# 48 instead of 40 tokens through the row experts of a hybrid decoder layer, one-hots in one operation, parts of p made earlier

## The chip, the cores and the metric

The kernel runs on one core of a Trainium2 chip. The metric is device time in microseconds (us) of one execution; lower is better. The kernel before took 2658.15 us, the median of three runs (2655.53 to 2660.96).

## What is computed

One layer for 264 tokens (256 of a prompt, 8 samples) of width 2048, in fp32. Two mixers (a chunked SSD scan and a short gated convolution) and their projections give x1; then each token goes through a product-key expert layer, and at the end a gate with a projection of p:

```python
def peer(x, w_q, keys1, keys2, u_tab, v_tab):
    q = (xt @ w_q).reshape(n, PEER_HEADS, 2, PEER_DKEY // 2)
    t1, i1 = lax.top_k(einsum(q[:, :, 0], keys1), 16)
    t2, i2 = lax.top_k(einsum(q[:, :, 1], keys2), 16)
    ...
    top, pos = lax.top_k(cand, 16)
    gate = softmax(top)
    hid = gelu(einsum('td,thkd->thk', x, u_tab[idx]))
    return einsum('thk,thkd->td', gate * hid, v_tab[idx])

x2 = LN(ALPHA * x1 + peer(x1))
y = x2 + sigmoid(x2 @ ple_gate_w) * (p @ ple_proj_w)
```

There are 8 heads, 128 x 128 = 16384 experts, each one row of u and one of v, and every token picks 16 experts per head, 128 in all.

## The kernel before

Every product is made from a high and a low part (fp32r) of both operands: `split_w` (L138) casts a half block of weights to `whi` on ACT and subtracts it to `wlo` on DVE (L146), three half blocks ahead (LOOK). A weight block is two halves of 512 KB each, fetched on the SP queue. `col_block` serves plain projections with three matmuls of 264 columns for each of 16 weight tiles.

The experts are reached in two ways. For the first TD = T - NSP = 224 tokens all 16384 experts are computed: `pair_block` (L260) streams, for each of 16 weight tiles, 448 columns (high and low parts side by side) against `whi` and the 224 high ones against `wlo`. 128 such blocks over u give hidden values, which go to DRAM as `a_d` (`u_evac`); 128 over v, in 8 chunks of 16 blocks, multiply coefficients `co` into accumulators (`v_evac`). The gate of each token and expert is built as a matrix of 128 x 128 by one-hots: `gates` (L1138) makes, for four tokens, `o1` on POOL (L1150) and `o2` on DVE (L1151); `g_mm` multiplies them and ACT gathers 32 tokens in `gs`, which goes to DRAM as `g_d`. Before each v chunk, `prep` (L1278) loads `gl` from `g_d` and `al` from `a_d` for four sets k, multiplies them on DVE (L1288), casts on ACT (L1296) and subtracts on DVE (L1297) to make `co`. The first of them can only begin when all gates are made, since `to_v` (L1340) closes the pools of the selection and of the one-hots before it opens the pool for v.

For the other NSP = 40 tokens (32 of the prompt's end and the 8 samples) `sparse_experts` (L1178) gathers the rows themselves: 128 rows at a time, one gather per token slot and table, 40 of u and 40 of v. DVE multiplies a gathered tile `ug` with `x1s` (L1206), and later accumulates v rows into `x1s` (L1216). Tokens come in groups GR, of 32 and of 8; at a group's end 16 small matmuls with `fld` fold the rows (`yS`, L1222), and the next group's `x1s` is loaded from `x1_d` (L1201).

What sets the order: the program is written out by hand. Main loops issue blocks; `tick` (L162) after each half block runs background tasks, generators that yield their cost in us of DVE, in the order of the list `tasks`, until the tick's budget is used, or `("w", n)` to sleep n ticks. `defer` runs a function n ticks later. `Grid(n)` makes a task come back every n ticks: every 3 for a group of four gates, every STEP = 4 for a gathered row. `select_all` (L1086) selects for three sets of tokens t = 0, 1, 2 (the prompt's second half, the samples, the prompt's first half), sends the indices of the row tokens to DRAM (`send`), spawns `sparse_experts` after t = 1 and the gates of the second half after t = 0. A v chunk whose `co` are not yet issued makes the program run ticks without a block (`run_out`). At the end the parts of p (`pp`) come from `quad`, four buffers that `co` of every second chunk, the last one too, also uses.

```python
    def quad(name, dt=R):
        return pairs.tile([128, 8 * TW], dt, name=name, tag="pr", bufs=KB // 4)
...
            if c % 2:
                co = quad("co")[:, 0:8 * TD]
...
    pp = quad("pp")[:, 0:4 * T].rearrange("p (q a t) -> p q a t", q=2, a=2)
```

Of the kernel before, what the change touches and what calls it, by code (L numbers as in the profile page):

```python
# [10 lines left out]
F = mybir.dt.float32  # L11
R = mybir.dt.float32r
# [9 lines left out]
TW = T + 2  # L22
NSP = 40
TD = T - NSP
# [21 lines left out]
TB = 32  # L46
NB = TD // TB
GR = ((0, 32), (32, 8))


@with_exitstack
def hybrid_step(ctx: ExitStack, tc: tile.TileContext, xT, pT, w_in, w_dt, w_bs, w_bc, w_o, w_q, w_pg, w_pp,
# [1033 lines left out]
    def select_all():  # L1086
# [26 lines left out]

    sx_d = [dram.tile([128, n], U32, name=f"sx{g}_d") for g, (_, n) in enumerate(GR)]
    sg_d = [dram.tile([128, n], F, name=f"sg{g}_d") for g, (_, n) in enumerate(GR)]
    x1_d = dram.tile([NSP, D], F, name="x1_d")

    def send(sel, t, nh):

        k0, m = GR[t]  # L1120
# [6 lines left out]
        lo, hi = (n - m, n) if t == 0 else (0, n)  # L1127
        r, c = hi - lo, nh * TOPK // m

        def out(d):  # L1130
            return bass.AP(tensor=d.tensor, offset=d.offset, ap=[[m, r], [r * m, c], [1, m]])

        gp.dma_start(out=out(sx_d[t]), in_=ix[lo:hi].rearrange("p (c m) -> p c m", m=m))
        gp.dma_start(out=out(sg_d[t]), in_=sel[lo:hi, 2].rearrange("p (c m) -> p c m", m=m))

    GS = {}

    def gates(t0, n):  # L1138
        oh = P["oh"]
        grid = Grid()  # L1140
        for tt in range(t0, t0 + n, 4):
            b0, q0 = divmod(tt, TB)
            if q0 == 0:
                GS["t"] = oh.tile([128, 128, TB], F, name="gs", tag="gs", bufs=2)
            gs = GS["t"]
# [7 lines left out]
            if q0 + 4 == TB:  # L1153
                defer(8, lambda gs=gs, b0=b0: sy.dma_start(out=g_d[b0], in_=gs))
            yield 1.1
            yield grid(3)
# [21 lines left out]
    def sparse_experts():  # L1178
        jobs = [(tab, k0, n, c) for k0, n in GR for tab in (uR, vR) for c in range(k0, k0 + n)]
        rows = {}  # L1180

        def get(i):
            if i < len(jobs):
# [4 lines left out]
                rows[i] = t  # L1188

        yield ("w", 1)  # L1190
        for g, (k0, n) in enumerate(GR):
            gp.dma_start(out=sidx[:, k0:k0 + n], in_=sx_d[g])
            gp.dma_start(out=scf[:, k0:k0 + n], in_=sg_d[g])
# [77 lines left out]
    def load(k):  # L1271
        gl = vp.tile([128, NB, 4, TB], F, name="gl", tag="gl", bufs=2)
        gp.dma_start(out=gl, in_=g_d[:, :, 4 * k:4 * k + 4, :].rearrange("b p e t -> p b e t"))
        al = vp.tile([128, 4, TD], F, name="al", tag="al", bufs=2)
        gp.dma_start(out=al, in_=a_d[k])
        AL[k] = (al, gl)

    def prep(c):  # L1278

        for k in range(4 * c, 4 * c + 4):  # L1280
# [83 lines left out]
    for c in range(ECH):  # L1364
# [88 lines left out]
def _inputs(x_prompt, x_sample, p_prompt, p_sample, state_ssm, state_ssd_conv, state_shortconv,  # L1453
# [70 lines left out]
```

## Time and profile before

| | before |
|---|---|
| median of three runs | 2658.15 us |
| the profiled execution | 2656.88 us |
| its span, first to last instruction | 2655.1 us |
| TensorE busy (matmuls) | 2617.6 us, 99% |
| DVE busy | 2017.8 us, 76% |
| ACT busy | 1347.8 us, 51% |
| POOL busy | 621.7 us, 23% |
| HBM read and written | 616.93 and 41.87 MB, 248 GB/s |

Shares are means over stages with different loads, so the stages have to be looked at one by one. Times in the trace are us from the first instruction. The u blocks run from about 1145 to 1858, the v blocks from there to 2532, the projection of p and the statistics to 2554 and the last projection to the end. Matmuls are pipelined: their spans overlap, and the spacing of their starts is the time that each one takes. PE is TensorE, PEld its weight loads.

### The profile page before, as it was taken

How to read it: one execution, taken by the hardware profiler on the slowest of the kernel's cores; microseconds unless marked ns; L12 is line 12 of the kernel's file. 1: busy time of each engine (PE TensorE's matmuls, PEld its weight loads, DVE VectorE, ACT ScalarE, POOL GpSimd, SP SyncE). 2: the span in 40 equal slices, each digit the busy share in tenths (PEclk: the TensorE clock that was granted, in tenths of full speed). 3: DMA queues.
4: the chain of work that ended last, by engine and by line, in shares of the span. 5: the costliest groups of instructions: out<-in, count | busy, mean ns of one | idle time of the engine just before them, and what ended most of it. 6: DMA issues, size and time to landing. Idle time of an engine off the chain costs nothing.

```text
span 2655.1 us, 48788 instructions
## 1 busy us (share of the span) xinstructions
PE 2617.6 (99%) x18983; PEld 2539.3 (96%) x18983; DVE 2017.8 (76%) x3371; ACT 1347.8 (51%) x1896; POOL 621.7 (23%) x743
## 2 busy tenths in 40 slices
PE   8999999999999999999999999999899999999999
PEld 8999999999999999999999999999899989999989
DVE  8899965556445567899997777778889889776976
ACT  5665533454344445654656555556444434444563
POOL 2232200000000010100356686742232222000100
PEclk9999999999999999999999999999999999999999
DMA  7798755555655555566778898889999999877654
GB/s 236 214 303 269 245 170 179 181 169 189 182 178 181 181 177 178 178 194 201 230 240 314 304 334 320 313 326 383 365 360 366 335 335 372 279 249 235 201 172 134
DMA packets 198601, 662.02 MB, mean 249 GB/s; under 512 B 22472, under 2 KB 59960, under 8 KB 186936
## 3 DMA queue, kind: packets, MB, share of 16 engines
q1 hardware_dynamic: 156128, 510.17, 58.0%
q0 software_dynamic: 24224, 129.62, 13.3%
q10 hardware_dynamic: 18016, 19.10, 2.1%
q8 instruction: 148, 2.42, 0.4%
q14 instruction: 85, 0.70, 0.1%
HBM read 616.93 MB, written 41.87 MB: 248 GB/s over the span
## 4 chain that ended last, share of the span: by engine, by line
PE 88%; DVE 6%; issue 3%; DMA 2%; POOL 1%; ACT 0%; SPq 0%; DVEq 0%; POOLq 0%; ACTq 0%
PE mm L270 25%; PE mm L236 14%; PE mm L234 14%; PE mm L235 14%; PE mm L271 13%; DVE wlo L146 2%; PE mm L273 2%; PE gps L1162 2%; DMA w<-uT 0%; DMA al<-a_d 0%; DVE x1s L1216 0%; DMA x1s<-x_d 0%; POOL ug L1186 0%; DVE acc L1323 0%; PE scr L994 0%
## 5 line engine op out<-in xcount | busy, mean ns | idle before, releaser
L146 DVE TENSOR_TENSOR wlo<-w,whi 128x1024 fp32r<-128x1024 f32 x916 | 1118.0, 1224 | 438.6 <-ACT whi L145 435.7
L145 ACT CAST whi<-w 128x1024 fp32r<-128x1024 f32 x916 | 961.5, 1051 | 822.1 <-PE mm L235 288.6
L270 PE MATMUL mm<-co,whi 128*128 128x448 f32 x1920 | 620.1, 377 | 6.7 <-DVE co L1297 6.7
L270 PE MATMUL mm<-x,whi 128*128 128x448 f32 x1920 | 620.5, 378 | 0.0
L236 PE MATMUL mm<-x,wlo 128*128 128x264 f32 x1920 | 549.6, 286 | 2.7 <-DVE wlo L146 2.7
L234 PE MATMUL mm<-x,whi 128*128 128x264 f32 x1920 | 549.5, 286 | 0.2 <-ACT whi L145 0.2
L235 PE MATMUL mm<-x,whi 128*128 128x264 f32 x1920 | 547.1, 285 | 0.0
L271 PE MATMUL mm<-co,wlo 128*128 128x224 f32 x2048 | 529.8, 269 | 6.6 <-DVE wlo L146 6.6
L271 PE MATMUL mm<-x,wlo 128*128 128x224 f32 x2048 | 525.3, 267 | 4.0 <-DVE wlo L146 4.0
L271 PEld LDWEIGHTS mm<-co,wlo 128*128 128x128 f32 x2048 | 394.5, 193 | 11.5 <-DVE wlo L146 7.6
L271 PEld LDWEIGHTS mm<-x,wlo 128*128 128x128 f32 x2048 | 392.4, 192 | 8.5 <-DVE wlo L146 5.4
L270 PEld LDWEIGHTS mm<-co,whi 128*128 128x128 f32 x1920 | 365.4, 190 | 36.3 <-DVE co L1297 8.1
L270 PEld LDWEIGHTS mm<-x,whi 128*128 128x128 f32 x1920 | 362.0, 189 | 28.1 <-ACT sv L996 0.5
L236 PEld LDWEIGHTS mm<-x,wlo 128*128 128x128 f32 x1920 | 362.0, 189 | 3.2 <-DVE wlo L146 3.1
L234 PEld LDWEIGHTS mm<-x,whi 128*128 128x128 f32 x1920 | 363.0, 189 | 1.9 <-issue 1.4
L235 PEld LDWEIGHTS mm<-x,whi 128*128 128x128 f32 x1920 | 363.2, 189 | 0.0
L1150 POOL TENSOR_SCALAR o<-iot,slot,slot 128x128 f32<-128x128 f32 x224 | 277.8, 1249 | 73.6 <-PE gps L1162 69.3
L1186 POOL DMA_INDIRECT ug<-vR,sidx x40 | 70.6, 1766 | 256.8 <-DVE x1s L1216 207.9
L832 POOL CAST r1h<-r1gbh 128x2 fp32r<-128x2 f32 x16 | 5.2, 328 | 476.3 <-PE mm L236 476.3
L1256 ACT COPY as<-mm 128x224 f32<-128x224 f32 x128 | 43.9, 343 | 115.0 <-PE mm L273 115.0
L1206 DVE SCALAR_TENSOR_TENSOR ug<-ug,x1s 128x2048 f32<-128x2048 f32 x40 | 91.4, 2284 | 8.0 <-DMA x1s<-x_d 8.0
L1186 POOL DMA_INDIRECT ug<-uR,sidx x40 | 62.9, 1571 | 140.0 <-DVE ug L1206 130.6
(348 smaller groups left out, 3904.2 us busy)
## 6 DMA issues: line engine op xcount, KB each, us to landing
w<-uT SPq DMA_DIRECT2D x256, 512.0 KB, 4.9
w<-vP SPq DMA_DIRECT2D x256, 512.0 KB, 5.9
w<-w_in SPq DMA_DIRECT2D x240, 512.0 KB, 3.7
w<-w_bc SPq DMA_DIRECT2D x32, 512.0 KB, 3.5
w<-w_bs SPq DMA_DIRECT2D x32, 512.0 KB, 3.5
w<-w_o SPq DMA_DIRECT2D x32, 512.0 KB, 3.5
w<-w_q SPq DMA_DIRECT2D x32, 512.0 KB, 3.6
w<-w_pg SPq DMA_DIRECT2D x32, 512.0 KB, 4.2
```

The costliest lines, as they stand in the source:

```text
L145: ac.copy(hi, w)
L146: ve.tensor_tensor(lo, w, hi.bitcast(F), OP.subtract)
L234: te.matmul(ps, wh, xh[kb], start=(first and q == 0), stop=False)
L235: te.matmul(ps, wh, xl[kb], start=False, stop=False)
L236: te.matmul(ps, wl, xh[kb], start=False, stop=(last and q == n - 1))
L270: te.matmul(ps, hi[:, ws], xp[kb], start=(kb == 0), stop=False)
L271: te.matmul(ps[:, :TD], lo[:, ws], xp[kb][:, :TD], start=False, stop=False)
L273: te.matmul(ps, hi[:, ws], xp[kb], start=False, stop=True)
L1150: gp.tensor_scalar(o1[:, q], iot, slot[0][:, c], slot[2][:, c], OP.is_equal, OP.mult)
L1162: te.matmul(ps[:, q * 128:(q + 1) * 128], o2[:, q], o1[:, q], start=True, stop=True)
L1186: gp.indirect_dma_start(out=t, out_offset=None, in_=tab, in_offset=bass.IndirectOffsetOnAxis(ap=sidx[:, c:c + 1], axis=0))
L1206: ve.scalar_tensor_tensor(t, t, 1.0, x1s, OP.mult, OP.mult, accum_out=shid[:, c:c + 1])
```

## The change

NSP becomes 48, so TD is 216: six blocks of 32 tokens and one of 24 (TR), which get a DRAM tile of their own (`gr_d`). GR gets a third group of 8; a group now names its selection (0 or 1) and its rows in it. The 48 row tokens are the prompt's last 40 and the 8 samples. `sparse_experts` is put at the head of the tasks at the end of selection 0, and waits for the samples' indices before its 33rd gather. `o2` for four tokens is one operation, and the yield behind it is 0.7 and not 1.1. The parts of p are made by a task that is spawned with the last v chunk, in buffers of the row experts.

```diff
-NSP = 40
+NSP = 48
...
-NB = TD // TB
-GR = ((0, 32), (32, 8))
+NB, TR = divmod(TD, TB)
+GR = ((0, 32, 0, 88, 32), (32, 8, 0, 120, 8), (40, 8, 1, 0, 64))
...
-            if t == 1:
-                spawn(sparse_experts())
+            if t == 0:
+                tasks.insert(0, {"gen": sparse_experts(), "wait": clock["t"] + 1})
...
-                ve.tensor_scalar(o2[:, q], iot, slot[1][:, c], None, OP.is_equal)
+            ve.tensor_tensor(o2, iot[:, None, :].to_broadcast([128, 4, 128]),
+                             slot[1][:, tt:tt + 4, None].to_broadcast([128, 4, 128]), OP.is_equal)
...
-            yield 1.1
+            yield 0.7
             yield grid(3)
...
+            if i == 32:
+                while "sent1" not in DONE:
+                    yield ("w", 1)
+                index(1)
             get(i + 1)
...
-        gl = vp.tile([128, NB, 4, TB], F, name="gl", tag="gl", bufs=2)
-        gp.dma_start(out=gl, in_=g_d[:, :, 4 * k:4 * k + 4, :].rearrange("b p e t -> p b e t"))
+        gl = vp.tile([128, 4 * TD], F, name="gl", tag="gl", bufs=2)
+        m = gl[:, 0:4 * NB * TB].rearrange("p (b e t) -> p b e t", b=NB, e=4)
+        r = gl[:, 4 * NB * TB:].rearrange("p (e t) -> p e t", e=4)
+        gp.dma_start(out=m, in_=g_d[:, :, 4 * k:4 * k + 4, :].rearrange("b p e t -> p b e t"))
+        gp.dma_start(out=r, in_=gr_d[:, 4 * k:4 * k + 4, :])
...
-            ve.tensor_tensor(av, av, gl.rearrange("p b e t -> p e b t"), OP.mult)
+            ve.tensor_tensor(av, av, m.rearrange("p b e t -> p e b t"), OP.mult)
+            ve.tensor_tensor(ar, ar, r, OP.mult)
...
+    def ple_parts():
+        pi = lp.tile([128, D], F, name="pi", tag="ug", bufs=2)[:, 0:2 * T].rearrange("p (q t) -> p q t", q=2)
+        gp.dma_start(out=pi, in_=pT)
+        pp = lp.tile([128, D], R, name="pp", tag="x1s", bufs=1)[:, 0:4 * T].rearrange("p (a q t) -> p a q t", q=2, a=2)
+        yield ("w", 4)
+        ac.copy(pp[:, 0], pi)
+        ve.tensor_tensor(pp[:, 1], pi, pp[:, 0].bitcast(F), OP.subtract)
...
             while "sparse" not in DONE:
                 tick(1.1)
+            spawn(ple_parts())
...
-    pp = quad("pp")[:, 0:4 * T].rearrange("p (q a t) -> p q a t", q=2, a=2)
-    for q in range(2):
-        t = block("pin")
-        gp.dma_start(out=t, in_=pT[:, q, :])
-        ac.copy(pp[:, q, 0], t)
-        ve.tensor_tensor(pp[:, q, 1], t, pp[:, q, 0].bitcast(F), OP.subtract)
```

Since a task list sets the order, these edits move instructions on every engine. Three places follow, with the names' buffer numbers.

POOL at the start of the gathers, before: behind selection 1 and behind 15 groups of `o1` (the last one stands here), the indices of both groups are loaded, then the first gather `ug` and the rows `x1s` are issued. L1150 is `o1`, L1192 and L1193 are the loads of the indices and gates, L1186 is a gather.

```order
L1150 TENSOR_SCALAR o1_17414<-iot_77,slot0_14370,slot2_14372 128x128 x4
L1192 DMA sidx_84<-sx0_d_13063 128x32
L1193 DMA scf_85<-sg0_d_13065 128x32
L1192 DMA sidx_84<-sx1_d_13064 128x8
L1193 DMA scf_85<-sg1_d_13066 128x8
L1186 DMA ug_17458<-uR,sidx_84 128x2048
L1201 DMA x1s_17460<-x1_d_13067 32x2048 x4
```

And in the change, where L1132 are the writes of the indices, L1188 is a gather and L1151 is `o1`:

```order
L1132 DMA sg1_d_13068<-sel0_15349 8x16x8
L1195 DMA sidx_84<-sx0_d_13064 128x32
L1196 DMA scf_85<-sg0_d_13067 128x32
L1195 DMA sidx_84<-sx1_d_13065 128x8
L1196 DMA scf_85<-sg1_d_13068 128x8
L1188 DMA ug_16027<-uR,sidx_84 128x2048
L1207 DMA x1s_16029<-x1_d_13070 32x2048 x4
L1188 DMA ug_16034<-uR,sidx_84 128x2048
L1151 TENSOR_SCALAR o1_16075<-iot_77,slot0_14373,slot2_14375 128x128 x4
```

The gathers stand ahead of the first `o1` of all, directly behind the writes of the indices that they read.

DVE at the seam from u to v, before: from the last block over u (L1257) to the first one over v (L1321). L1297 makes a `co`, L1216 adds a gathered row, L1288 multiplies `al` by `gl`.

```order
L1257 TENSOR_TENSOR as_22125<-mm_22129,as_22125 128x224
L1297 TENSOR_TENSOR co_22178<-al_21855,co_22178 128x4x224
L1216 SCALAR_TENSOR_TENSOR x1s_17460<-ug_22067,scf_85,x1s_17460 128x2048
L1288 TENSOR_TENSOR al_22071<-al_22071,gl_22069 128x896
L1297 TENSOR_TENSOR co_22191<-al_22071,co_22191 128x4x224
L1216 SCALAR_TENSOR_TENSOR x1s_17460<-ug_22176,scf_85,x1s_17460 128x2048
L146 TENSOR_TENSOR wlo_22201<-w_22152,whi_22200 128x1024
L146 TENSOR_TENSOR wlo_22227<-w_22198,whi_22226 128x1024
L1321 SCALAR_TENSOR_TENSOR acc_21527<-acc_21527,mm_22197 128x448
```

In the change the same stretch begins so (L1267 for L1257, L1301 and L1302 for L1288, L1311 for L1297, L1226 for L1216):

```order
L1267 TENSOR_TENSOR as_21940<-mm_21944,as_21940 128x216
L1301 TENSOR_TENSOR al_21883<-al_21883,gl_21880 128x4x192
L1302 TENSOR_TENSOR al_21883<-al_21883,gl_21880 128x4x24
L1226 SCALAR_TENSOR_TENSOR x1s_16029<-ug_21878,scf_85,x1s_16029 128x2048
L1311 TENSOR_TENSOR co_22009<-al_21883,co_22009 128x4x216
L1226 SCALAR_TENSOR_TENSOR x1s_16029<-ug_21991,scf_85,x1s_16029 128x2048
L1301 TENSOR_TENSOR al_21996<-al_21996,gl_21993 128x4x192
L1302 TENSOR_TENSOR al_21996<-al_21996,gl_21993 128x4x24
L1311 TENSOR_TENSOR co_22034<-al_21996,co_22034 128x4x216
L1226 SCALAR_TENSOR_TENSOR x1s_16029<-ug_22007,scf_85,x1s_16029 128x2048
```

The third and the fourth `co` follow in the same three rows, with one L1226 between them and one behind, and then two `wlo` and the first v block. All four of the first chunk's `co` stand behind the last u block; before, it was the difference of the third and the fourth.

DVE at the switch to the new third group of rows, in the change, at the end of the third v chunk (L1337 adds a v block, L1237 takes the folded group, L1216 multiplies the first rows of the next by the new `x1s`):

```order
L1337 TENSOR_TENSOR acc_22053<-mm_24458,acc_22053 128x432
L1311 TENSOR_TENSOR co_24509<-al_24261,co_24509 128x4x216
L1237 SCALAR_TENSOR_TENSOR x1sp_83<-x1sp_83,yS_24504 128x16x8
L147 TENSOR_TENSOR wlo_24548<-w_24481,whi_24547 128x1024
L1216 SCALAR_TENSOR_TENSOR ug_24358,shid_86<-ug_24358,x1s_24525 128x2048
L147 TENSOR_TENSOR wlo_24571<-w_24545,whi_24570 128x1024
```

Before, only the switch from the group of 32 to that of 8 stands there.

## Rows read from the trace of the kernel before

**Rows 1.** Stretches: window, length, busy us of PE, PEld, DVE, ACT, POOL, clock, DMA, GB/s.

```profile
650.00:700.00 50.00, 50.00 (x413) 50.00 (x412) 22.56 (x21) 19.73 (x22) 0.00 (x0) 1.00 0.59 180
...
1250.00:1300.00 50.00, 47.85 (x296) 45.24 (x295) 46.14 (x79) 28.44 (x40) 8.29 (x9) 0.97 0.72 231
...
1800.00:1850.00 50.00, 49.38 (x314) 46.79 (x313) 40.11 (x42) 32.02 (x48) 13.36 (x11) 1.00 1.01 391
...
2000.00:2050.00 50.00, 49.80 (x315) 47.07 (x315) 45.97 (x40) 22.72 (x22) 15.25 (x12) 1.00 0.93 361
...
GB/s 236 214 303 269 245 170 179 181 169 189 182 178 181 181 177 178 178 194 201 230 240 314 304 334 320 313 326 383 365 360 366 335 335 372 279 249 235 201 172 134
```

**Rows 2.** Waits of PE, whole span: us in total, times, longest.

```profile
PE mm L271 <- DVE wlo L146: 10.6, 7, 4.4
PE mm L270 <- DVE co L1297: 6.7, 5, 3.8
```

**Rows 3.** Timeline of PE in the tail: start, us, instruction, [idle before <- releaser].

```profile
2532.12 0.37 PE L273 MATMUL mm<-co,whi 128*128 128x448 f32 x1
...
2538.57 0.59 PE L1391 MATMUL mm<-pp,whi 128*128 128x264 f32 x1 [6.08 <-ACT pp L1378]
...
2554.10 0.29 PE L234 MATMUL mm<-r,whi 128*128 128x266 f32 x1
```

**Rows 4.** Timeline of DVE and PE at the seam from u to v.

```profile
1858.73 1.08 DVE L1297 TENSOR_TENSOR co<-al,co 128x896 fp32r<-128x896 f32 x1
1859.73 2.35 DVE L1216 SCALAR_TENSOR_TENSOR x1s<-ug,scf,x1s 128x2048 f32<-128x2048 f32 x1
1861.99 1.09 DVE L1288 TENSOR_TENSOR al<-al,gl 128x896 f32<-128x896 f32 x1
1864.09 1.09 DVE L1297 TENSOR_TENSOR co<-al,co 128x896 fp32r<-128x896 f32 x1 [1.00 <-ACT co L1296]
...
1859.87 0.47 PE L270 MATMUL mm<-co,whi 128*128 128x448 f32 x1 [1.08 <-DVE co L1297]
...
1865.23 0.74 PE L270 MATMUL mm<-co,whi 128*128 128x448 f32 x1 [3.84 <-DVE co L1297]
```

**Rows 5.** Timeline of PE in a u block, with one group of gates.

```profile
1700.94 0.26 PE L271 MATMUL mm<-x,wlo 128*128 128x224 f32 x1
1701.04 0.38 PE L270 MATMUL mm<-x,whi 128*128 128x448 f32 x1
1701.25 0.27 PE L271 MATMUL mm<-x,wlo 128*128 128x224 f32 x1
1701.35 1.06 PE L1162 MATMUL gps<-o,o 128*128 128x128 f32 x8
1702.17 0.46 PE L270 MATMUL mm<-x,whi 128*128 128x448 f32 x1
```

**Rows 6.** Timeline of PE at the group switch (last matmuls of v blocks, fold matmuls).

```profile
2110.61 3.65 PE L1222 MATMUL yS<-fld,x1s 128*128 128x32 f32 x32
...
2120.58 0.37 PE L273 MATMUL mm<-co,whi 128*128 128x448 f32 x1
...
2125.65 0.38 PE L273 MATMUL mm<-co,whi 128*128 128x448 f32 x1
...
2133.10 0.56 PE L271 MATMUL mm<-co,wlo 128*128 128x224 f32 x1 [4.36 <-DVE wlo L146]
...
2137.19 0.60 PE L273 MATMUL mm<-co,whi 128*128 128x448 f32 x1
...
2277.66 0.96 PE L1222 MATMUL yS<-fld,x1s 128*128 128x8 f32 x8
```

**Rows 7.** Timeline of DVE and POOL at the same switch.

```profile
2129.61 2.29 DVE L1206 SCALAR_TENSOR_TENSOR ug<-ug,x1s 128x2048 f32<-128x2048 f32 x1 [7.99 <-DMA x1s<-x_d]
...
2114.56 4.03 POOL L1201 DMA_DIRECT2D x1s<-x_d  x8 [17.36 <-PE yS L1222]
```

**Rows 8.** Landing times of the loads of `al` (L1275) and of gathers (L1186).

```profile
DMA to landing us min/median/max: 3.3/10.4/14.0
...
DMA to landing us min/median/max: 6.9/9.2/15.6
```

More of the change, by code (lines that the diff above doesn't have):

```diff
@@ L954, in hybrid_step @@
     g_d = dram.tile([NB, 128, 128, TB], F, name="g_d")
+    gr_d = dram.tile([128, 128, TR], F, name="gr_d")
     DONE = {}
@@ L1111, in select_all @@
         yield from gates(0, PT // 2)
-    sx_d = [dram.tile([128, n], U32, name=f"sx{g}_d") for g, (_, n) in enumerate(GR)]
-    sg_d = [dram.tile([128, n], F, name=f"sg{g}_d") for g, (_, n) in enumerate(GR)]
+    sx_d = [dram.tile([128, n], U32, name=f"sx{g}_d") for g, (_, n, _, _, _) in enumerate(GR)]
+    sg_d = [dram.tile([128, n], F, name=f"sg{g}_d") for g, (_, n, _, _, _) in enumerate(GR)]
     x1_d = dram.tile([NSP, D], F, name="x1_d")
     def send(sel, t, nh):
-        k0, m = GR[t]
         sp = P["sp"]
@@ L1126, in send @@
         ve.tensor_copy(ix[:n], fx[:n])
[L1127 to L1134, printed above, removed]
+        for g, (_, m, tile_, lo, r) in enumerate(GR):
+            if tile_ == t:
+                c = nh * TOPK // m
+                for d, src in ((sx_d[g], ix), (sg_d[g], sel[:, 2])):
+                    gp.dma_start(out=bass.AP(tensor=d.tensor, offset=d.offset, ap=[[m, r], [r * m, c], [1, m]]),
+                                 in_=src[lo:lo + r].rearrange("p (c m) -> p c m", m=m))
+        DONE["sent%d" % t] = True
     GS = {}
@@ L1142, in gates @@
             b0, q0 = divmod(tt, TB)
+            tb = TB if b0 < NB else TR
             if q0 == 0:
                 GS["t"] = oh.tile([128, 128, TB], F, name="gs", tag="gs", bufs=2)
-            gs = GS["t"]
+            gs = GS["t"].rearrange("p e t -> p (e t)")[:, 0:128 * tb].rearrange("p (e t) -> p e t", t=tb)
             o1 = oh.tile([128, 4, 128], F, name="o1", tag="o1", bufs=3)
@@ L1150, in gates @@
                 gp.tensor_scalar(o1[:, q], iot, slot[0][:, c], slot[2][:, c], OP.is_equal, OP.mult)
-                ve.tensor_scalar(o2[:, q], iot, slot[1][:, c], None, OP.is_equal)
+            ve.tensor_tensor(o2, iot[:, None, :].to_broadcast([128, 4, 128]),
+                             slot[1][:, tt:tt + 4, None].to_broadcast([128, 4, 128]), OP.is_equal)
             defer(6, lambda o1=o1, o2=o2, gs=gs, q0=q0: g_mm(o1, o2, gs, q0))
-            if q0 + 4 == TB:
-                defer(8, lambda gs=gs, b0=b0: sy.dma_start(out=g_d[b0], in_=gs))
-            yield 1.1
+            if q0 + 4 == tb:
+                defer(8, lambda gs=gs, b0=b0: sy.dma_start(out=g_d[b0] if b0 < NB else gr_d, in_=gs))
+            yield 0.7
             yield grid(3)
@@ L1178, in sparse_experts @@
     def sparse_experts():
-        jobs = [(tab, k0, n, c) for k0, n in GR for tab in (uR, vR) for c in range(k0, k0 + n)]
+        jobs = [(tab, k0, n, c) for k0, n, _, _, _ in GR for tab in (uR, vR) for c in range(k0, k0 + n)]
         rows = {}
@@ L1188, in get, with index @@
                 rows[i] = t
+        def index(t):
+            for g, (k0, n, tile_, _, _) in enumerate(GR):
+                if tile_ == t:
+                    gp.dma_start(out=sidx[:, k0:k0 + n], in_=sx_d[g])
+                    gp.dma_start(out=scf[:, k0:k0 + n], in_=sg_d[g])
         yield ("w", 1)
-        for g, (k0, n) in enumerate(GR):
-            gp.dma_start(out=sidx[:, k0:k0 + n], in_=sx_d[g])
-            gp.dma_start(out=scf[:, k0:k0 + n], in_=sg_d[g])
+        index(0)
         get(0)
@@ L1338, in residual @@
                 yield ("w", 1)
+    def ple_parts():
[5 more added lines that the diff above has]
+        ve.tensor_tensor(pp[:, 1], pi, pp[:, 0].bitcast(F), OP.subtract)
+        for q in range(2):
+            p_h.append(pp[:, 0, q])
+            p_l.append(pp[:, 1, q])
+        yield 0.7
     def to_v():
@@ L1488, in _inputs @@
         iota=np.tile(np.arange(128, dtype=np.float32), (128, 1)),
-        fold=np.concatenate([np.tile(np.eye(n), (128 // n, 1)) for _, n in GR], 1).astype(np.float32),
+        fold=np.concatenate([np.tile(np.eye(g[1]), (128 // g[1], 1)) for g in GR], 1).astype(np.float32),
     )
```

8 lines of the change are left out of this document (3 added, 5 removed).

## Prediction

> **What bounds the kernel now.** I read the busy time of stretches first. In the stretch of plain projections TensorE is busy for all of 50.00 us and issues 413 matmuls of 264 columns, 0.121 us each, with DVE at less than half [rows 1]. In the expert stages it is busy nearly all the time too, but with company: DVE 46.14 and 45.97 of 50 us in the stretches at 1250 and 2000, the DMA engines at 0.93 to 1.01 of their time with 361 to 391 GB/s from 1800 on [rows 1]. Then what TensorE waits for: over the whole span 10.6 us for DVE's low parts of the weights and 6.7 us for DVE's coefficients `co` [rows 2]; the other large wait, 6.08 us, stands in the tail [rows 3]. So this kernel is bound by TensorE's columns, with DVE and the DMA engines close behind in the expert stages. Fewer columns are worth their full time wherever DVE and DMA keep up, and every place where TensorE runs out of prepared operands costs its wait and then some: after the 3.84 us wait the first 448-column matmul shows 0.74 us and not 0.38 [rows 4, 5], which is the lower of the clock's two levels, 1.2 and not 2.4 GHz.
>
> **Columns.** TD falls from 224 to 216, so each `pair_block` streams 16 x (432 + 216) columns and not 16 x (448 + 224): 384 fewer. In order of time, a 448-column matmul is followed after 0.21 us, a 224-column one after 0.10 us [rows 5], and a whole block takes 5.07 us (2120.58 to 2125.65, [rows 6]), 0.47 ns a column, much as the 264-column stretch gives (0.121 us / 264 = 0.46 ns). By proportion a block loses 5.07 x 24 / 672 = 0.181 us; there are 128 blocks over u and 128 over v, so **-46.3 us**. The bounds: 0.417 ns a column, which is 2.4 GHz, gives -41; only the 16 columns of the wide matmul counting gives -31 (a rival below). I take the proportional price because three widths lie on one line through zero.
>
> **Gates.** 54 groups of four tokens and not 56. A group holds TensorE from 1701.35 to 1702.17, 0.82 us [rows 5]: **-1.6 us**. The one `o2` operation in place of four lies on DVE in a stretch in which nothing waits for it; I cost it at nothing, and the yield that falls from 1.1 to 0.7 only lets the other tasks have more of a tick.
>
> **Parts of p.** Now the last v matmul starts at 2532.12, and the p projection waits 6.08 us for its operand: the tile comes from the same four buffers as `co` of the last chunk, so the load cannot start before the last v block has ended. The out projection begins at 2554.10 [rows 3], 21.8 us after the last v matmul has streamed its 0.21 us. The work between is 96 matmuls at 0.121 us and four of the statistics, about 12.6 us. With the parts made at the start of the last chunk, in two tiles that the row experts have left, TensorE goes straight on: **-9.2 us**, the wait and the low clock behind it. Next late would be the statistics, issued after three of the four quarters of the projection, some 9 us after the last block; DVE and ACT need about 5 us for the last block's chain, so I expect no new wait. Bounds: 0 to -10.
>
> **The third group of row tokens.** 48 rows are 96 gathers and not 80. In the program's order they begin with the first selection's end, and the last is issued at the same v block as before (chunk 4, block 9); so the load on DVE and the DMA engines in the v stage stays as it is, and the extra 16 lie in the u stage, 2.3 us of DVE each, in ticks that have room (they come out of the same budget). But a group has fixed costs. The switch from the group of 32 to that of 8 shows them: DVE sits 7.99 us for the rows `x1s`, which POOL writes with 16 DMAs that can only start when the group's matmuls have read the old tile [rows 7]; TensorE runs out of low parts for 4.36 us, and the block takes 11.54 us (2125.65 to 2137.19), 6.5 over [rows 6]. The new third group adds one more such switch, with the gathered product again directly behind the tile's load on DVE, and one more set of fold matmuls in four pieces of 0.95 us [rows 6]. **+10.3 us**; bounds +4 (the fold alone) to +13.
>
> **The seam from u to v.** This is where the change loses. Selection and gates now share their budget with the gathers, so the last gates end 22 ticks later in the program and the pools for v open 20 ticks later: 6 half blocks before u ends, not 26. Before, three of the first chunk's four `co` were made by then, and TensorE waited 1.08 and 3.84 us for the rest, behind one gathered row and one product [rows 4]. In the new order all four stand between the last u block and the first v block on DVE, with four gathered rows among them. DVE alone: four row operations 4 x 2.26 (1859.73 to 1861.99), four products 4 x 1.2 (the split of `gl` into two adds some 0.2), four differences of 1.0, three waits of 1.0 for ACT's cast [rows 4] = 20.8 us, where 6.4 stand now (1858.73 to 1865.1). So at least +14.5. But the second, third and fourth loads each wait for a buffer or for POOL, which is held by a gather that waits for DVE; gathers land 9.2 us after issue, coefficients 10.4 (medians; 6.9 and 3.3 at best [rows 8]). With 8 us for a load, since the weights pause, and 7.5 for a gather, the last `co` comes some 29 us after the last u block, +22; with 11.4 us a load, +28. I take **+20 us**, the low clock at the restart included, nearer to the waits than to DVE's bare sum since the DMA engines were full in this stretch [rows 1].
>
> **DVE with less slack.** Blocks get 3.6% shorter, DVE's work does not, and the first gather now goes out directly behind the indices it needs, so DVE will stand for the first rows, as it did for 7.99 us at the switch [rows 7], of which half reached TensorE. **+4 us** for all of this, between 0 and +10.
>
> Sum: -46.3 - 1.6 - 9.2 + 10.3 + 20 + 4 = -22.8 against the profiled execution's 2656.9 us, 2634; the median of the three runs is 1.3 higher, so I say **2635 us**. A measurement of this kernel can tell about 0.2%, 5.3 us, from no change.
>
> **Rivals.**
> - *Weight loads set the pace of the narrow matmuls.* 32 matmuls of only 32 columns (f32) took 3.65 us, 0.114 each [rows 6]: there the columns are not what counts. If fp32r has a floor at the 0.10 us which the 224-column matmuls show, 216 columns are no faster and a block gains 16 x 16 x 0.47 ns only, -31 in all: **2651**. Against it: 0.10 for 224 and 0.121 for 264 lie in the ratio of the columns. The Trainium skill, page "TensorE: Matmul & The Clock Gate", section "LDWEIGHTS (loading the stationary operand)", gives a load about P/1.2 ns, 107 ns for 128 columns, which is this rival's floor; the spacing of 0.10 us in the rows is already slightly below it, so the trace speaks rather against.
> - *The seam is short*: loads land as at their best and DVE's bare sum rules, +14, and DVE's slack suffices: **2625**.
> - *The seam is long*, +28, and each restart drags the next blocks, +6: **2649**.
> - *The DMA engines become the bound in v (slower).* While gathers run, a block needs two weight halves of 0.52 MB, half a gather of 1.05 MB and a quarter of 0.88 MB of coefficients: 1.79 MB. At 4.89 us that is 367 GB/s, where the v stretch now shows 361 at 0.93 [rows 1]. Chunks 0 to 4 are 80 blocks; 14.5 us of the gain lie there. Without it the sum is -8.3, so the change loses from 5.17 us a block on, a limit of 346 GB/s. At 335 GB/s, the lowest two slices of the v stage on the page [rows 1], a block would take 5.36, +23: **2672**. Against it: 391 GB/s at 1.01 [rows 1].
>
> **How the numbers follow.** Forecast 0.50, weight floor 0.13, short seam 0.15, long seam 0.13, DMA bound 0.09. Faster by over 0.2% means below 2653: the forecast, the short seam and most of the weight floor and the long seam, 0.83. Within 0.2%: what is left of these two, 0.08. Slower: the DMA bound, 0.09. The range reaches from the low edge of the short seam (seam +12, no allowance, second switch +8), 2616, to the high edge of the long one and the foot of the DMA case, 2658.
>
> **What would show it.** A v block at 4.89 us between undisturbed last matmuls, and u blocks likewise; 204 and 100 ns between starts. If the narrow one stays at 0.10 and above and the block at 4.95, the floor is there. A wait of TensorE for `co` of 15 to 28 us in sum at the seam; two waits of DVE for `x1s` near 8 us in the v stage, each with some 4 us of TensorE behind it; no wait for `pp`. The prediction is wrong if v blocks in chunks 0 to 4 spread beyond 5 us with `whi` waiting for weights (DMA), if the seam costs no more than now, or if new waits for `wlo` appear all through the u stage, where I put the extra gathers at nothing.

## The result and the profile after

The change makes the kernel slower: 2682.06 us (median of four runs, 2679.95 to 2686.26) against 2659.36 us (four runs of the kernel before on the same chip, 2655.53 to 2660.96), a ratio of 1.0089, 95% interval 1.0072 to 1.0107. The forecast was 2635, a gain of 0.9%. The profiled execution took 2681.55 us, its span 2679.8, 24.7 more than the span before.

Its page and its waits of TensorE (us in total, times, longest; line numbers of the changed kernel, where L271 is the matmul against `whi`, L272 the one against `wlo`, L274 a block's last one):

```profile
PE 2605.1 (97%) x18999; PEld 2549.7 (95%) x18999; DVE 2039.8 (76%) x3258; ACT 1343.0 (50%) x1894; POOL 739.7 (28%) x802
...
PE mm L272 <- DVE wlo L147: 29.5, 13, 7.8
PE mm L271 <- DVE co L1311: 15.1, 4, 6.5
PE mm L271 <- issue: 8.3, 1, 8.3
...
PE yS L1232 <- DVE x1s L1226: 4.1, 1, 4.1
```

Against [rows 2], the waits for `wlo` rise from 10.6 to 29.5 us, those for `co` from 6.7 to 15.1, and 8.3 us at the first v block come on top, which the view puts down to "issue"; the 6.08 us for `pp` [rows 3] are gone. Busy time of TensorE falls by 12.5 us only. To see where the 24.7 us arise I take the starts of each block's last matmul; they cut the span into five parts. A block is the time from one such start to the next, and I call a block "clean" when it is as long as the 21st shortest of its stage, my measure for one that nothing held up:

| us | to the last matmul of the first u block | u | seam: last u to first v block | v | after | span |
|---|---|---|---|---|---|---|
| before | 1148.3 | 707.6 | 11.5 | 664.8 | 123.0 | 2655.1 |
| after | 1149.9 | 710.7 | 33.5 | 670.1 | 115.6 | 2679.8 |

A clean block takes 4.927 us in u and 4.933 in v; before it took 5.033 and 5.047. So 128 blocks should have made u some 14 us shorter and v some 15, and yet both grew.

**The seam.** Timeline of PE and DVE from the last u block to the end of the first v block:

```profile
1860.58 0.37 PE L274 MATMUL mm<-x,whi 128*128 128x432 f32 x1
1869.25 0.70 PE L271 MATMUL mm<-co,whi 128*128 128x432 f32 x1 [8.30 <-issue]
1878.37 0.73 PE L271 MATMUL mm<-co,whi 128*128 128x432 f32 x1 [6.53 <-DVE co L1311]
1886.06 0.73 PE L271 MATMUL mm<-co,whi 128*128 128x432 f32 x1 [5.06 <-DVE co L1311]
1891.98 0.73 PE L271 MATMUL mm<-co,whi 128*128 128x432 f32 x1 [3.29 <-DVE co L1311]
1894.04 0.59 PE L274 MATMUL mm<-co,whi 128*128 128x432 f32 x1
...
1871.89 2.35 DVE L1226 SCALAR_TENSOR_TENSOR x1s<-ug,scf,x1s 128x2048 f32<-128x2048 f32 x1 [2.75 <-DMA ug<-vR,sidx]
1875.15 0.96 DVE L1301 TENSOR_TENSOR al<-al,gl 128x768 f32<-128x768 f32 x1 [0.91 <-DMA al<-a_d]
...
1882.84 0.96 DVE L1301 TENSOR_TENSOR al<-al,gl 128x768 f32<-128x768 f32 x1 [2.26 <-DMA al<-a_d]
```

The block stops four times, once for each of the first chunk's `co` (the first stop, which the view puts down to "issue", ends as DVE ends the first `co`, which it makes from 1868.10 for 1.05 us); one gathered row stands between every two of them on DVE, and DVE itself waits for a gather and for loads of `al`. Each wait is followed by a 432-column matmul of 0.70 to 0.73 us, twice the 0.37 of the row above: the stretch from 1850 to 1900 has a mean granted clock of 0.62, between the two levels of 1.2 and 2.4 GHz:

```profile
1300.00:1350.00 50.00, 43.83 (x277) 42.37 (x277) 36.05 (x50) 24.66 (x32) 44.63 (x26) 0.93 0.86 290
...
1850.00:1900.00 50.00, 25.39 (x107) 22.72 (x108) 36.08 (x32) 22.46 (x35) 17.23 (x21) 0.62 0.85 314
2000.00:2050.00 50.00, 42.44 (x257) 41.12 (x258) 42.81 (x46) 18.14 (x19) 14.70 (x14) 0.90 0.89 327
```

**The start of the gathers and the group switches.** The other two rows of this view are the places where much of the rest goes: TensorE busy for 43.83 and 42.44 of 50 us. The first is the start of the gathers, the second the switch from the group of 32 to that of 8. POOL, DVE and PE at the start, then at the switch:

```profile
1287.74 0.58 POOL L1132 DMA_DIRECT2D sx_d<-ix  x1 [71.48 <-DVE ix L1127]
...
1296.36 1.04 POOL L1188 DMA_INDIRECT ug<-uR,sidx  x1 [1.61 <-DMA sidx<-sx_d]
1297.41 2.01 POOL L1207 DMA_DIRECT2D x1s<-x_d  x4
...
1311.78 2.29 DVE L1216 SCALAR_TENSOR_TENSOR ug<-ug,x1s 128x2048 f32<-128x2048 f32 x1 [8.41 <-DMA x1s<-x_d]
...
1315.27 0.55 PE L272 MATMUL mm<-x,wlo 128*128 128x216 f32 x1 [6.17 <-DVE wlo L147]
...
1987.44 5.71 POOL L1207 DMA_DIRECT2D x1s<-x_d  x11 [15.02 <-PE yS L1232]
1995.42 2.83 POOL L1207 DMA_DIRECT2D x1s<-x_d  x5 [2.28 <-DMA x1s<-x_d]
...
2004.06 2.29 DVE L1216 SCALAR_TENSOR_TENSOR ug<-ug,x1s 128x2048 f32<-128x2048 f32 x1 [11.25 <-DMA x1s<-x_d]
...
2007.56 0.55 PE L272 MATMUL mm<-co,wlo 128*128 128x216 f32 x1 [7.79 <-DVE wlo L147]
```

In both places DVE's next instruction is a product with `x1s`, and the rows of `x1s` are still on their way: ordered from 1297.41 on they are there at 1311.78, and from 1987.44 (which is when the fold matmuls release the tile) at 2004.06. DVE sits for 8.41 and 11.25 us with the next `wlo` behind the product, and TensorE runs out of low parts. The new second switch, at 2151 to 2180, shows the same: 12.19 us of DVE and 6.99 us of TensorE.

### The profile page after: what moved, and what is told of

The parts are those of the page before. It is cut to its first block, busy times and chain, and to the rows that moved or that the text cites. A ratio compares the mean times of both kernels' runs of the same rounds, so it can differ in the third digit from the quotient of the medians.

```text
span 2679.8 us, 48780 instructions
## 1 busy us (share of the span) xinstructions
PE 2605.1 (97%) x18999; PEld 2549.7 (95%) x18999; DVE 2039.8 (76%) x3258; ACT 1343.0 (50%) x1894; POOL 739.7 (28%) x802
## 3 DMA queue, kind: packets, MB, share of 16 engines
q0 software_dynamic: 27664, 146.49, 15.1%
## 4 chain that ended last, share of the span: by engine, by line
PE 82%; POOL 6%; DMA 5%; DVE 4%; issue 2%; ACT 1%; SPq 0%; DVEq 0%; ACTq 0%; POOLq 0%
PE mm L271 22%; PE mm L237 15%; PE mm L235 15%; PE mm L236 15%; PE mm L272 11%; POOL o L1151 5%; DMA w<-uT 2%; PE mm L274 1%; DVE wlo L147 1%; PE gps L1164 1%; DMA x1s<-x_d 1%; POOL ug L1188 1%; DMA ug<-uR,sidx 1%; DMA al<-a_d 1%; PE yS L1232 0%
## 5 line engine op out<-in xcount | busy, mean ns | idle before, releaser
L271 PE MATMUL mm<-co,whi 128*128 128x432 f32 x1920 | 613.8, 377 | 23.4 <-DVE co L1311 15.1
L271 PE MATMUL mm<-x,whi 128*128 128x432 f32 x1920 | 610.4, 375 | 1.1 <-ACT whi L146 1.1
L272 PE MATMUL mm<-co,wlo 128*128 128x216 f32 x2048 | 524.6, 266 | 14.8 <-DVE wlo L147 14.8
L272 PE MATMUL mm<-x,wlo 128*128 128x216 f32 x2048 | 521.3, 265 | 14.8 <-DVE wlo L147 14.7
L272 PEld LDWEIGHTS mm<-co,wlo 128*128 128x128 f32 x2048 | 397.6, 194 | 17.4 <-DVE wlo L147 15.6
L272 PEld LDWEIGHTS mm<-x,wlo 128*128 128x128 f32 x2048 | 393.7, 192 | 21.0 <-DVE wlo L147 19.0
L271 PEld LDWEIGHTS mm<-co,whi 128*128 128x128 f32 x1920 | 368.3, 192 | 42.8 <-DVE co L1311 16.5
L271 PEld LDWEIGHTS mm<-x,whi 128*128 128x128 f32 x1920 | 364.0, 190 | 17.6 <-ACT whi L146 1.5
L1151 POOL TENSOR_SCALAR o<-iot,slot,slot 128x128 f32<-128x128 f32 x216 | 354.1, 1646 | 1.6
L1216 DVE SCALAR_TENSOR_TENSOR ug<-ug,x1s 128x2048 f32<-128x2048 f32 x48 | 110.3, 2297 | 44.2 <-DMA x1s<-x_d 31.8
L1188 POOL DMA_INDIRECT ug<-vR,sidx x48 | 78.7, 1640 | 219.9 <-DVE x1s L1226 167.5
L1188 POOL DMA_INDIRECT ug<-uR,sidx x48 | 72.7, 1514 | 162.1 <-DVE ug L1216 133.6
L1226 DVE SCALAR_TENSOR_TENSOR x1s<-ug,scf,x1s 128x2048 f32<-128x2048 f32 x45 | 105.5, 2345 | 2.7 <-DMA ug<-vR,sidx 2.7
```

The lines of the kernel that those rows point to most:

```text
L271: te.matmul(ps, hi[:, ws], xp[kb], start=(kb == 0), stop=False)
L272: te.matmul(ps[:, :TD], lo[:, ws], xp[kb][:, :TD], start=False, stop=False)
L1188: gp.indirect_dma_start(out=t, out_offset=None, in_=tab, in_offset=bass.IndirectOffsetOnAxis(ap=sidx[:, c:c + 1], axis=0))
L1216: ve.scalar_tensor_tensor(t, t, 1.0, x1s, OP.mult, OP.mult, accum_out=shid[:, c:c + 1])
L1226: ve.scalar_tensor_tensor(x1s, t, scf[:, c:c + 1], x1s, OP.mult, OP.add)
```

## Experiments

Two things were to be settled: why a block lost 0.11 us and not 0.18, and whether the seam, the start and the switches are the order's doing. For the first, three kernels change the columns of one matmul in the kernel before.

**Narrow matmul of 128 columns** (of 224), one run.

```diff
-                te.matmul(ps[:, :TD], lo[:, ws], xp[kb][:, :TD], start=False, stop=False)
+                te.matmul(ps[:, :128], lo[:, ws], xp[kb][:, :128], start=False, stop=False)
```

> The kernel before, with the matmul against wlo streaming 128 of its 224 columns (so 96 tokens lose the product with the low part of the weights). Theory A, the slot of this matmul is held by the load of the next weights: the loads of the weights start 0.108 us apart there with 224 columns and with 216, so they will with 128; a clean block stays at 5.03 to 5.05 us and the time within 5 us of the kernel before, 2657. Theory B, the prediction's proportional price: 16 x 96 columns x 0.47 ns = 0.72 us less a block, over 256 blocks -185 us, 2472.

Measured: 2657.93 us, against 2657.52 for the kernel before (median of 11 runs). 4096 matmuls lost 43% of their columns and nothing was gained. Starts of weight loads in a v block (PEld), of the kernel before, then of the changed kernel, then of this one:

```profile
2400.37 0.19 PEld L270 LDWEIGHTS mm<-co,whi 128*128 128x128 f32 x1
2400.48 0.19 PEld L271 LDWEIGHTS mm<-co,wlo 128*128 128x128 f32 x1
2400.68 0.19 PEld L270 LDWEIGHTS mm<-co,whi 128*128 128x128 f32 x1
```

```profile
2401.34 0.19 PEld L271 LDWEIGHTS mm<-co,whi 128*128 128x128 f32 x1
2401.45 0.19 PEld L272 LDWEIGHTS mm<-co,wlo 128*128 128x128 f32 x1
2401.64 0.19 PEld L271 LDWEIGHTS mm<-co,whi 128*128 128x128 f32 x1
```

```profile
2401.27 0.19 PEld L270 LDWEIGHTS mm<-co,whi 128*128 128x128 f32 x1
2401.38 0.19 PEld L271 LDWEIGHTS mm<-co,wlo 128*128 128x128 f32 x1
2401.58 0.19 PEld L270 LDWEIGHTS mm<-co,whi 128*128 128x128 f32 x1
```

The load of `wlo` follows that of `whi` by 0.11 us in all three: in the median 108 to 109 ns, with 224, 216 and 128 columns alike. This is the short slot; the long one, from `wlo` to `whi`, is 206 ns with 448 columns and 200 with 432. 16 x (206 + 108) = 5.02 us and 16 x (200 + 108) = 4.93 us, the clean blocks. So 16 columns of the wide matmul count, 8 of the narrow one do not. The starts of the matmuls themselves don't show this slot. In this kernel's timeline of PE a narrow one is followed by the next wide one after 0.06 us, and that by the next narrow one after 0.25:

```profile
2401.27 0.22 PE L271 MATMUL mm<-co,wlo 128*128 128x128 f32 x1
2401.33 0.42 PE L270 MATMUL mm<-co,whi 128*128 128x448 f32 x1
2401.58 0.22 PE L271 MATMUL mm<-co,wlo 128*128 128x128 f32 x1
```

In the medians that is 60 and 255 ns, in the kernel before 103 and 212: the sum stays at 315. That it is the load of the weights itself which holds the slot, and not another fixed cost of a matmul, agrees with these rows but isn't separated by them, since every matmul here comes with a load.

**Narrow matmul of 256 columns**, one run; the same line with `:256`.

> The kernel before, with the matmul against wlo streaming 256 columns and not 224 (the first 32 tokens get a product of wlo with the low part added). Theory A (a floor of 0.108 us): the columns count again above the floor; 264 columns have 0.121 us, so 256 some 0.118, and a block grows by 16 x 0.010 = 0.16 us, +41 us, 2698. Theory B (0.47 ns a column): 16 x 32 x 0.47 ns = 0.24 us a block, +62 us, 2719.

Measured: 2669.21, +11.7 us. The short slot is 118 ns, as expected, and the clean block 5.14 us; but the long slot fell from 206 to 204 ns, and the waits for `co` and `wlo` shrank as blocks became longer (7.5 us for `wlo`, 10.6 before; 5.2 for `co`, 6.7 before), so the time rose by less than either theory said. Above the floor columns count again.

**Wide matmul of 384 columns** (of 448), one run.

```diff
-                    te.matmul(ps, hi[:, ws], xp[kb], start=(kb == 0), stop=False)
+                    te.matmul(ps if kb == 0 else ps[:, :384], hi[:, ws], xp[kb] if kb == 0 else xp[kb][:, :384], start=(kb == 0), stop=False)
...
-                    te.matmul(ps, hi[:, ws], xp[kb], start=False, stop=True)
+                    te.matmul(ps[:, :384], hi[:, ws], xp[kb][:, :384], start=False, stop=True)
```

> The kernel before, with 15 of a block's 16 matmuls against whi streaming 384 of 448 columns (so 64 tokens lose most of the product of the low part of x or of co with whi). Theory A (the wide matmul goes by its columns, 6 ns for 16 as 448 to 432 showed, 0.39 ns each): 15 x 64 x 0.39 ns = 0.37 us less a block, 4.67 us, -96 us, 2561, if DVE and the DMA engines keep up; where they don't, a wait for wlo shows it and the gain is smaller. Theory B (0.47 ns a column): -0.45 us a block, -115 us, 2542.

Measured: 2605.95 us, -51.6, about half of what either theory gave, though the clean block is even shorter than expected, 4.61 us (long slot 179 ns: 27 ns for 64 columns, 0.42 each). 256 blocks x 0.43 us would be 110 us; 58 of them are missing. Waits of TensorE:

```profile
PE mm L271 <- DVE wlo L146: 27.4, 25, 6.1
PE mm L270 <- DVE co L1297: 18.8, 5, 4.6
PE mm L1391 <- ACT pp L1378: 10.2, 1, 10.2
PE mm L270 <- ACT whi L145: 5.2, 2, 3.6
```

`wlo` 10.6 to 27.4, `co` 6.7 to 18.8, `pp` 6.1 to 10.2, `whi` from 0 to 5.2: 38.2 us more in these four than before (61.6 and 23.4), since blocks 9% shorter meet a DVE whose work stayed. The mean granted clock of the span is 0.986, before 0.993; by estimate that is at most some 18 us (0.7% of 2604), so the two together can account for nearly all that is missing.

**Parts of p alone**: the kernel before with `ple_parts` in place of the two `pin` blocks, three rounds.

```diff
             while "sparse" not in DONE:
                 tick(1.1)
+            spawn(ple_parts())
...
-    pp = quad("pp")[:, 0:4 * T].rearrange("p (q a t) -> p q a t", q=2, a=2)
```

> The kernel before, with the parts of p made by the task of the change and nothing else changed. My theory: the wait of 6.08 us for pp goes and the low clock behind it, -7 to -9 us, 2650. Rival: the statistics come next and take the time back, within 3 us of the kernel before.

Measured: 2649.57 us against 2657.52, ratio 0.9968 (0.9958 to 0.9979). In its timeline the out projection starts 12.85 us after the last v matmul, where [rows 3] show 21.98:

```profile
2530.96 0.38 PE L273 MATMUL mm<-co,whi 128*128 128x448 f32 x1
2543.81 0.29 PE L234 MATMUL mm<-r,whi 128*128 128x266 f32 x1
```

**The row experts spawned after selection 1**, as before; the rest of the change stays. Three rounds.

```diff
-            if t == 0:
-                tasks.insert(0, {"gen": sparse_experts(), "wait": clock["t"] + 1})
+            if t == 1:
+                spawn(sparse_experts())
```

> The changed kernel, with the row experts spawned after selection 1 as in the kernel before; all else of the change stays. My theory: the seam of 33.47 us and the block of 14.79 us at the first rows come from the gathers that share the selection's and the gates' ticks, so both go back to what the kernel before shows (about 11 us, and 9 or less): -22 for the seam and -6 to -10 for the start, 2682 - 30 = 2652, the two group switches still there (two blocks of 9 to 16 us each, now in later chunks). Rival: the seam is long because gl is loaded and multiplied in two pieces; then it stays near 30 us and the time above 2672.

Measured: 2638.23 us, ratio to the kernel before 0.9932 (0.9915 to 0.9949). One edit of four lines is worth 44 us (42 by the two ratios to the kernel before) and turns the change into a gain. Parts of its span: 1148.9, u 702.7, seam 4.9, v 662.6, after 116.0. Its timeline of PE at the seam shows three last matmuls one clean block apart, and the stretch around it:

```profile
1851.64 0.37 PE L274 MATMUL mm<-x,whi 128*128 128x432 f32 x1
1856.59 0.37 PE L274 MATMUL mm<-co,whi 128*128 128x432 f32 x1
1861.54 0.37 PE L274 MATMUL mm<-co,whi 128*128 128x432 f32 x1
```

```profile
1850.00:1900.00 50.00, 48.82 (x316) 46.86 (x315) 43.23 (x41) 22.13 (x23) 16.84 (x14) 1.00 0.96 361
```

There is no seam left, with `gl` still loaded and multiplied in two pieces, so the rival falls. It is better even than before (11.5): selection and gates, which have their ticks back and shorter one-hots, let the pools for v open sooner. The first load of `gl`, which follows on that, goes out 82.7 us before the last matmul over u (1768.98), before 57.7 (1798.19), in the change 11.9 (1848.73). Two blocks of 11.7 and 13.8 us at the switches remain.

**First products 8 ticks later**, early start kept. Three rounds.

```diff
-            yield grid(STEP)
+            yield grid(STEP + (8 if tab is uR and c == k0 else 0))
```

> The changed kernel, with the first product of each of the three groups 8 ticks later than its rows x1s are ordered (all later jobs shift by as much); the early start stays. My theory: DVE's waits for x1s (8.41, 11.25 and 12.19 us) hold up the wlo queued behind them, and that is what the start and the two switches cost; with the delay DVE doesn't wait for x1s, the blocks of 14.79, 15.88 + 14.83 and 8.50 + 14.55 us fall to 6 to 9 each, -20 to -30 us, 2657; the seam stays at 33 us. Rival: the switch costs the yS matmuls, the 16 DMAs and the gather's landing wherever they stand, so the loss only moves by some blocks: 2678 to 2686.

Measured: 2657.54 us, ratio to the kernel before 0.9999 (0.9987 to 1.0012), 24.5 less than the changed kernel: the expected sum. Its places are only half the expected ones. Of the span's 28.8, u gives 12.8 (the first rows' block 10.06 and not 14.79), the seam 11.1 (22.4 and not 33.5, as gates get ahead meanwhile: the first load of `gl` goes out at 1804.61, 43.3 us before u ends) and v 5.1: two switch blocks of 12.33 and 13.35 us remain. POOL and DVE at the second of them:

```profile
2183.99 0.51 POOL L1207 DMA_DIRECT2D x1s<-x_d  x1 [0.16 <-issue]
2184.80 1.02 POOL L1188 DMA_INDIRECT ug<-uR,sidx  x1 [0.30 <-DMA x1s<-x_d]
...
2195.61 2.29 DVE L1216 SCALAR_TENSOR_TENSOR ug<-ug,x1s 128x2048 f32<-128x2048 f32 x1 [9.52 <-DMA ug<-uR,sidx]
```

The group's first product still stands for 9.52 us. The view names a gathered row, but this product's own was ordered well before the fold; what was under way is the last of the 16 loads of `x1s`, which by the trace landed at 2195.43, and, behind it, the next row, which landed at 2199.05, after the product had begun. So the delay worked at the start and was too short at the switches; the next kernel shows why.

**Both edits.** Three rounds.

> The changed kernel with both edits: row experts after selection 1, and the first product of a group 8 ticks later. My theory: the two act in different places and add up, -30 and -15 to -20 (the start counts once), 2682 - 48 = 2634, so faster than both kernels; the gathers then end some 8 ticks ahead of the last chunk. Rival: gathers that end this late leave DVE or the DMA engines no room in chunks 5 and 6, and the v blocks there grow by 0.1 to 0.3 us; 2640 to 2650.

Measured: 2638.08 us, ratio to the kernel before 0.9922 (0.9905 to 0.9938): no better than the late start alone. u fell to 691.4 us, v rose to 673.8, with two blocks of 16.5 and 16.3 us. POOL, DVE and PE at the first of them:

```profile
2081.23 5.05 POOL L1207 DMA_DIRECT2D x1s<-x_d  x10 [23.05 <-PE yS L1232]
...
2092.27 0.50 POOL L1207 DMA_DIRECT2D x1s<-x_d  x1 [0.54 <-DMA x1s<-x_d]
...
2104.52 2.29 DVE L1216 SCALAR_TENSOR_TENSOR ug<-ug,x1s 128x2048 f32<-128x2048 f32 x1 [12.94 <-DMA x1s<-x_d]
...
2108.01 0.55 PE L272 MATMUL mm<-co,wlo 128*128 128x216 f32 x1 [9.47 <-DVE wlo L147]
```

From the first load of `x1s` to its last landing it takes 23.3 us, more than nine ticks of a half block (4.93 / 2 us); POOL issues ten loads in a row and from then on waits for an earlier one to land before most. And the 8 ticks were not 8: `Grid` counts from the last due time, which the fold's own ticks had passed by, so about 5 were left, as in the kernel above.

**Groups of 32 and 16**, with both edits. Three rounds. The 8 prompt tokens take partitions 0 to 63 of a gather, the samples 64 to 127; `fold` is made to match.

```diff
-GR = ((0, 32, 0, 88, 32), (32, 8, 0, 120, 8), (40, 8, 1, 0, 64))
+GR = ((0, 32), (32, 16))
+PARTS = ((0, 0, 0, 88, 32, 32), (1, 0, 0, 120, 8, 8), (1, 64, 1, 0, 64, 8))
...
-                for q in range(128 // n):
-                    gp.dma_start(out=x1s[q * n:(q + 1) * n], in_=x1_d[ks])
+                for q in range(128 // n if n == 32 else 16):
+                    if n == 32:
+                        gp.dma_start(out=x1s[q * n:(q + 1) * n], in_=x1_d[ks])
+                    else:
+                        gp.dma_start(out=x1s[q * 8:(q + 1) * 8], in_=x1_d[32:40] if q < 8 else x1_d[40:48])
```

> The changed kernel with both edits, and with the two groups of 8 tokens made one of 16 (same 96 gathers, one switch and one set of fold matmuls less, a narrower set of fold operands). My theory: a switch with the delayed product costs 2 to 4 us in fold matmuls and interrupted blocks, so 2 to 4 us less than the kernel with both edits alone, about 2631. Rival: a switch costs nothing once DVE doesn't wait: the same as that kernel within 1.5 us.

Measured: 2616.47 us, ratio to the kernel before 0.9844 (0.9828 to 0.9860), 21.6 less than with three groups, and faster than both kernels. Both theories were too small, since both took the delay to work. In the kernel with three groups the last switch still shows blocks of 6.7, 16.3 and 6.5 us, 14.7 in sum over clean ones, which are gone here, and so are two blocks of 5.8 beside the first of them, another 1.8. The other 5 us I can't place: the trace of this kernel is of its longest execution, 2626.23 us, and its span is only 12.0 shorter than that of three groups.

**The same with a full 12 ticks at the switch.** Three rounds.

```diff
+            if i and tab is uR and c == k0:
+                grid.t = clock["t"]
```

> The kernel of e8 with the first product of the second group a full 12 ticks after its rows x1s are ordered (in e8 the grid made up for the fold's ticks, so that some 5 were left and DVE still waited 13.73 us for x1s; the rows landed 23 us after the last fold matmul, which is 9 to 10 ticks). My theory: that wait of DVE goes, the v block of 17.3 us falls to 5 or 6, -11 us, 2605. Rival: the rows land later the more of POOL's and DMA's work gets done in between, DVE still waits some us: 2610 to 2617.

Measured: 2617.24 us, ratio to the kernel before 0.9836 (0.9815 to 0.9858): no further gain, a miss. DVE doesn't wait for `x1s` at the switch any more, but the loads that were held up behind it now come late themselves:

```profile
2113.51 0.96 DVE L1308 TENSOR_TENSOR al<-al,gl 128x768 f32<-128x768 f32 x1 [4.21 <-DMA al<-a_d]
...
2115.83 0.55 PE L273 MATMUL mm<-co,wlo 128*128 128x216 f32 x1 [3.74 <-DVE wlo L148]
```

The block at the switch is 11.6 us long, with a wait for `al` behind 16 loads of `x1s` on POOL's queue: the loads of `gl` and `al` that follow on them are themselves held up by loads of `x1s` that haven't landed.

```profile
2100.45 0.84 POOL L1292 DMA_DIRECT2D gl<-g_d  x1 [1.07 <-DMA x1s<-x_d]
```

So here a part of the switch's cost lay in what stands behind those loads. That it always does isn't shown, and the last kernel below speaks against it. A second tile for `x1s`, loaded ahead, might be the remedy; it wasn't tried.

**The one-hots alone**: the kernel before with the single `o2` and the yield of 0.7. Three rounds.

> The kernel before with o2 for four tokens as one DVE operation and the yield behind it 0.7 instead of 1.1, nothing else. My theory (the prediction's): it lies on DVE where nothing waits for it, within 3 us of the kernel before. Rival: DVE is the engine that sets the late gates and gathers in u, so the shorter one-hots give 3 to 8 us.

Measured: 2655.43 us against 2658.13, ratio 0.9990 (0.9977 to 1.0004), no difference that can be told. Its seam is shorter, 8.2 and not 11.5 us.

**40 tokens with all the other edits**: parts of p, the single `o2`, the switch of the 12-tick kernel. Three rounds.

> The kernel before (40 tokens by row, groups of 32 and 8) with the parts of p, the single o2 and the delayed first products of e10, so everything of e10 but the 8 tokens more. My theory: -8 for the parts, -8 to -11 for the switch, 2658 - 18 = 2640; e10 is then 26 us of columns faster less what 16 gathers more cost, so 20 to 35 us below this one. Rival: the 8 tokens more are worth little, and e8 and e10 have their time from the other edits: this one within 10 us of e10.

Measured: 2638.04 us, ratio 0.9918 (0.9898 to 0.9939). The same with 48 tokens is 20.8 us faster. The two traces are 17.0 us apart: u gives 12.2 (708.6 and 696.4), the seam 2.8 (7.8 and 4.9) and v only 4.6 (655.7 and 651.1), though its clean blocks gain 15. What takes back the rest is not spread over the 16 gathers more. It lies behind the switch, where the kernel with 48 tokens has blocks of 6.7, 11.6 and 6.5 us, 10.0 over clean ones; here, with the same 12 ticks and the same 16 loads of `x1s`, the first three blocks behind the fold take 5.05 us each, and none before the next fold takes over 5.7. So with 12 ticks a switch can be free but for its fold matmuls; in the kernel with 48 tokens it fell on the loads of the next chunk's `gl` and `al`.

## Why the prediction was wrong, point by point

The sum forecast was -22.8, the span shows +24.7: 47.5 apart. By its terms:

- **Columns, -46.3 forecast, -28 measured** (128 x 0.106 in u, 128 x 0.114 in v by the clean blocks): +18. This is the step that failed first, "three widths lie on one line through zero": 0.10 us for the narrow matmul was read as its columns and was a floor. I read it from the start of the narrow matmul to that of the wide one behind it, which is not its slot, as the kernel with 128 columns shows (60 ns there, with the sum of the two unchanged); the starts of the loads show 108 ns. The rival that I gave 0.13 was right, its price of -31 nearly so. The rule I set aside there, the Trainium skill's page "TensorE: Matmul & The Clock Gate", section "LDWEIGHTS (loading the stationary operand)", about P/1.2 ns, which is 107 for 128 columns, agrees with the 108 ns measured at 224, 216 and 128 columns. It is the spacing that agrees: the rows give each load 0.19 us.
- **The first group switch, 0 forecast, +10.4 measured.** Its two long blocks and those beside them lie 22.7 us over clean ones, in the kernel before 12.3. This is the second step that failed. I priced the new switch and left the old one as it was; in the change DVE waits 11.25 us there and not 7.99, and the fold's first piece itself waits 4.09 us. Shorter blocks and gathered rows in another phase may be why; no run separates them.
- **The third group, +10.3 forecast, +13.2 measured** (blocks of 8.50 and 14.55 us). The mechanism, DVE standing for `x1s`, was right. Merging the two groups of 8, with the late start and the delay, gave 21.6.
- **The seam, +20 forecast, +20.4 measured** by the excess over clean blocks of the seam and the first v blocks behind it (22.0 by the table, for the seam alone). Right in mechanism and size; and the late start alone, which took it away, shows it to be the price of the early start. The rival "short seam" fell.
- **DVE with less slack, +4 forecast, about +19 measured**, by what the other terms leave: +9 at the first rows, the rest nearly all small waits in the u stage that I didn't follow one by one, so their cause is open. The step that failed at the start is "of which half reached TensorE": of DVE's 8.41 us TensorE waited 6.17, and with the low clock behind it its block is 9.0 us longer than others with a group of gates.
- **Parts of p, -9.2 forecast, -7.4 in the change and -8.9 alone** by the stage behind v: right. **Gates, -1.6 forecast, -2.7 measured**: a block with one group is 0.89 us over a clean one, before 0.91, and there are 54 groups and not 56. **o2**, at nothing: right, though it does shorten the seam.
- **DMA bound in v**: didn't happen. The blocks between switches stay at 4.93 to 4.95 us. The time came out on the slow side all the same, and no rival of mine stood there with the right mechanism: the early start and the switches were both in my sum, and their cost was not bounded as one thing that could outweigh the columns. With the columns right the sum would have been -5, and the first switch, +10.4, would have turned its sign. The low edge of the range doesn't follow from its terms, which give 2621 and not 2616; the miss is at the other edge.

What the runs add: the idea of the change was worth having. 48 tokens by row beat 40 by 20.8 us when the rest is equal, and with the late start and groups of 32 and 16 the kernel takes 2616.5 us, 1.6% less than before and 2.4% less than the change (2616.47 / 2682.06 = 0.976).

## What to carry to other kernels

Before columns are priced, look at the spacing of the weight loads in the trace: where two matmuls of different widths alternate, the shorter may lie on a floor, and cutting its columns buys nothing (128 and 224 columns took the same time here). In a program whose order is written out, an edit that starts a background task earlier takes its ticks from whatever the next stage is waiting for; ask which task holds that stage's first operand. And a product placed directly behind the load of its operand, with other engines' operands queued behind it, can cost the landing time of that load, at every place where it stands; count the places, and those that stand there already.

## What the runs showed of the hardware that was not expected

- A matmul with its own weights of 128 x 128 took a slot of 108 ns with 128, 216 or 224 columns; with 256 columns 118, with 264 122, with 384 179, with 432 200 and with 448 206 ns (spacing of weight loads, medians, at the higher clock).
- 16 loads of 64 KB each on POOL's queue, 8 partitions a load, took 16.6 us (in the change, 1987.44 to 2004.06) to 23.3 us from the first issue to the last landing in the v stage.
- Blocks 9% shorter brought 1.9% of the time (51.6 of 2657.5 us) where their 256 x 0.43 us are 4.1%: 38.2 us went into longer waits for work of other engines that had been hidden, and the mean granted clock fell from 0.993 to 0.986.
